# Three of sixteen pairs of k tiles in the MLP's second product done with seven block products, with the left sums on VectorE

## The chip, the cores and the metric

The kernel runs on one core of one Trainium2 chip. The metric is the device time of one execution in microseconds, as the median of several runs. A core has TensorE (matmuls; its weight loads run on a queue of their own), VectorE, ScalarE, GpSimd and SyncE, which issues most of the loads. Matmuls accumulate in PSUM, which has eight banks of 128 x 512 float32 each.

## The reference

A decoder block on 256 tokens of width 2048: a sparse attention and a Mamba-2 mixer merged by gates, an output projection, and then an MLP with 8192 hidden channels. Only the MLP's second product is done in another way here:

```python
h2 = rms_norm(x, norm2_g[l])
x = x + jnp.square(jax.nn.relu(h2 @ w_up[l])) @ w_down[l]
```

`w_up` is 2048 x 8192, `w_down` 8192 x 2048, all in float32, and the answer is wanted close to float32 accuracy.

## The kernel before

**Three matmuls for one product.** The matrices are float32; TensorE is given each operand as a high part (a copy rounded to fp32r by ScalarE, `hi`) and a low part (what is left, by VectorE, `lo`). A product of a 128 x 128 left tile by a 128 x 512 right tile is then three matmuls into the same PSUM bank: high by high, high by low, low by high. `split` (line 107) makes the two parts of a weight tile of 128 x 1024; `load` (line 115) brings the tile from HBM on SyncE's queue, into four buffers in turn; `hi` and `lo` have three buffers each.

**The MLP.** It goes in two halves of 4096 hidden channels: `up(0)`, `down(0)`, `up(1)`, `down(1)`. `up(h)` makes the hidden activations `u` (32 k tiles of 128 channels by 256 tokens) in four passes of 1024 channels. `down(h)` multiplies `u` by the matching rows of `w_down` in two passes, c2 = 0 and 1, of 1024 output columns each, over all 32 k tiles. Between a pass of `up` and the next, tasks from a queue (`u_task`) transpose the activations through an auxiliary bank; `pump` hands them out.

**The passes of `up` are mixed.** `mixed` (line 964) takes the k tiles in pairs, by the letters of `UP = "NSNSNSNN"`. With two k tiles (k), two token tiles (t) and two column halves, a pair is a 2 x 2 by 2 x 2 block product. A pair "N" takes eight products, 24 matmuls: `pieces_n` splits two weight tiles and no sums of weights are needed. A pair "S" takes seven products, 21 matmuls, by a Strassen-like scheme: `pieces_s` (line 936) needs four sums of weight blocks (`t13`, `t24`) and splits seven blocks, and the left side needs sums of the left blocks too, which `left` (line 860) makes. Seven banks q[1] to q[7] collect the products, and `combine` (line 1001) adds them up to the four output blocks at the end of the pass. In `up` the left operands (`xa`) are made once, by `norm_task`, with the left sums on GpSimd, and used by all eight passes.

**The passes of `down` are plain.** `down` (line 1079) calls `gemm_a` (line 148): for each k tile it makes the parts of `u` on the fly (`u_st`, line 1072: one ScalarE copy and one VectorE subtraction of 128 x 256, tile `uhl`), splits one weight tile and issues 4 products, 12 matmuls, into four banks. At the end of a pass one VectorE addition per bank adds the residual `xn`, into `xn` itself in `down(0)` (line 1093) and into a tile `o` in `down(1)` (line 1096), from where it goes out to HBM.

**Order.** The tile framework orders the instructions of each engine by a simulated timeline, and decides at that time which of a pool's buffers a tile gets. Seven PSUM banks are main banks, one is the auxiliary bank. Each engine then works its own list strictly in order.

Of the kernel before, what the change touches and what calls it, by code (L numbers as in the profile page):

```python
# [10 lines left out]
F32 = mybir.dt.float32  # L11
# [8 lines left out]
P = 128  # L20
# [15 lines left out]
UP = "NSNSNSNN"  # L36
NB = 32
# [9 lines left out]
def body(tc, x, x_t, vectors, taps, w_in, dt_bias, a_log, d_skip, bias_t, w_att_branch,  # L47
# [10 lines left out]
    with ctx:  # L58
# [905 lines left out]
        def mixed(kinds, w, k0, c0, operands, rate):  # L964

            q = {i: main_bank() for i in (1, 6, 7, 2, 5, 3, 4)}
            left_of = {i: sum(1 if kind == "S" else 2 * (i in LEFT_N) for kind in kinds)
# [9 lines left out]
            for j, kind in enumerate(kinds):  # L977
                hi, lo = operands(j)
                kk = k0 + 2 * j
                if kind == "S":  # L980
# [3 lines left out]
                else:  # L984
                    ws = pieces_n(w, kk, c0)
                    last = j == len(kinds) - 1
                    todo = [(i, k) for k in range(2) for i in LEFT_N]
                    if last:
                        todo.sort(key=lambda x_: list(LEFT_N).index(x_[0]))
                    for i, k in todo:  # L990
                        s_, c = LEFT_N[i]
                        s_ += 3 * k
# [8 lines left out]
        def combine(q, out_, before=None):  # L1001
# [6 lines left out]
            def with_(x_, t, c, op=OP.add):  # L1008
                if before is not None:
                    (nc.gpsimd if before[1] else v).tensor_tensor(x_, x_, before[0](t, c), op=op)  # L1010
                return x_
# [60 lines left out]
        def u_st(kk):  # L1072
            if kk == 24:
                drain()
            t = fp.tile([P, 512], F32R, name=nm("uhl"), tag="uhl", bufs=4)
            a.copy(t[:, :S], u[:, kk])
            v.tensor_tensor(t[:, S:], u[:, kk], t[:, :S].bitcast(F32), op=OP.subtract)
            return t

        def down(h):  # L1080
            for c2 in range(2):
                banks = [[main_bank(), main_bank()] for _ in range(2)]

                def d_pieces(kk):
                    hi, lo = split(load(w_down, h * MH // P + kk, 1, c2 * 1024, 1024),
                                   [P, 1, 1024])
                    return 1, hi, lo
                for t, c in gemm_a(d_pieces, MH // P, u_st, banks, 2500,
                                   tail=2 if h and c2 else 0):
                    c0 = c2 * 1024 + c * 512  # L1090
                    x_ = xn[:, t, c0:c0 + 512]
                    if h == 0:
# [56 lines left out]
```

## Time and profile before

| | |
|---|---|
| median of 3 runs | 1988.07 us (1987.48 to 1989.61) |
| the profiled execution | 1988.68 us, its span 1987.0 us |
| TensorE busy (matmul) / weight loads | 1973.6 us, 99% / 1641.5 us, 83% |
| VectorE busy | 1418.3 us, 71% |
| ScalarE busy | 1041.4 us, 52% |
| mean granted TensorE clock | 0.999 |
| up(0), down(0), up(1), down(1) begin at | 1281, 1458, 1634 and 1806 us of the span |

A busy time is the time in which an engine has an instruction under way. A matmul's shown length of some 0.39 us overlaps with the next one, so the step from one start to the next, not the length, says what a matmul costs. "Idle before, releaser" is the time an engine stood still ahead of an instruction and what it waited for.

### The profile page before, as it was taken

The numbers are of one execution on the slowest core, as the hardware profiler recorded it, in microseconds if no ns is written. First come the engines' busy times: TensorE is split into PE (matmuls) and PEld (weight loads), VectorE is DVE, ScalarE is ACT, GpSimd is POOL, SyncE is SP. The second block draws the span as 40 slices with busy tenths as digits, with TensorE's granted clock in tenths as the row PEclk, the third lists the DMA queues.
The fourth block names the chain that finished last, engine by engine and source line by source line (L and its number), as shares of the span: only waits on it lengthen the run. The fifth ranks groups of instructions, "written<-read, shape, count | busy, mean of one in ns | idle before, by whom it ended". The sixth has DMA issues, their size and how long they took to land.

```text
span 1987.0 us, 26274 instructions
## 1 busy us (share of the span) xinstructions
PE 1973.6 (99%) x9473; PEld 1641.5 (83%) x9473; DVE 1418.3 (71%) x2335; ACT 1041.4 (52%) x1566; POOL 56.8 (3%) x110
## 2 busy tenths in 40 slices
PE   8999999999999999999999999999999999999999
PEld 7878888888888888888888888778888888888887
DVE  7868656568888887888656565688855668886565
ACT  6555555444455554554554545566655445565553
POOL 2000000000000000000000000110000000000000
PEclk9999999999999999999999999999999999999999
DMA  7645555566555555565565556556656665655664
GB/s 228 209 135 183 180 168 166 161 221 191 179 182 184 187 187 185 181 187 163 179 194 188 192 190 224 179 176 205 193 189 193 194 196 190 202 190 191 192 215 145
DMA packets 132227, 372.26 MB, mean 187 GB/s; under 512 B 18288, under 2 KB 18928, under 8 KB 131840
## 3 DMA queue, kind: packets, MB, share of 16 engines
q1 hardware_dynamic: 128704, 357.87, 56.5%
q0 software_dynamic: 3248, 12.65, 2.0%
q8 instruction: 74, 1.21, 0.2%
q14 instruction: 57, 0.47, 0.1%
q10 hardware_dynamic: 144, 0.06, 0.0%
HBM read 368.37 MB, written 2.16 MB: 186 GB/s over the span
## 4 chain that ended last, share of the span: by engine, by line
PE 96%; DVE 2%; ACT 1%; DMA 1%; issue 0%; POOL 0%; SPq 0%; DVEq 0%; ACTq 0%; POOLq 0%
PE mb L152 59%; PE mb L973 15%; PE mb L126 10%; PE mb L127 5%; PE ab L747 1%; PE ab L1058 1%; PE ab L457 1%; DVE lo L111 1%; DMA raw<-in_w_in_dram 0%; PE ab L766 0%; PE ab L691 0%; PE ab L739 0%; PE ab L711 0%; PE ab L551 0%; PE ab L576 0%
## 5 line engine op out<-in xcount | busy, mean ns | idle before, releaser
L111 DVE TENSOR_TENSOR lo<-raw,hi 128x1024 fp32r<-128x1024 f32 x640 | 781.8, 1224 | 475.3 <-ACT hi L110 474.2
L110 ACT CAST hi<-raw 128x1024 fp32r<-128x1024 f32 x640 | 671.5, 1052 | 730.3 <-PE mb L152 487.4
L152 PE MATMUL mb<-hi,h_hl 128*128 128x512 f32 x1408 | 444.1, 393 | 0.0
L152 PE MATMUL mb<-hi,uhl 128*128 128x512 f32 x1024 | 315.9, 389 | 0.0
L152 PEld LDWEIGHTS mb<-hi,h_hl 128*128 128x128 f32 x1408 | 263.2, 188 | 57.1 <-issue 3.4
L152 PE MATMUL mb<-lo,h_hl 128*128 128x512 f32 x704 | 278.1, 395 | 0.3 <-DVE lo L111 0.3
L973 PE MATMUL mb<-hi,xa 128*128 128x512 f32 x832 | 263.0, 392 | 2.6 <-DVE xn L919 2.2
L126 PE MATMUL mb<-h_hl,hi 128*128 128x512 f32 x768 | 262.5, 396 | 0.0
L152 PEld LDWEIGHTS mb<-hi,uhl 128*128 128x128 f32 x1024 | 192.3, 188 | 39.8
L127 PE MATMUL mb<-h_hl,lo 128*128 128x256 f32 x768 | 204.2, 286 | 0.0
L152 PE MATMUL mb<-lo,uhl 128*128 128x512 f32 x512 | 200.0, 391 | 0.0
L973 PEld LDWEIGHTS mb<-hi,xa 128*128 128x128 f32 x832 | 156.9, 189 | 35.8 <-ACT sq L922 2.6
L126 PEld LDWEIGHTS mb<-h_hl,hi 128*128 128x128 f32 x768 | 141.9, 188 | 30.6 <-issue 1.7
L973 PE MATMUL mb<-lo,xa 128*128 128x512 f32 x416 | 164.4, 395 | 0.2
L152 PE MATMUL mb<-hi,yhl 128*128 128x512 f32 x512 | 158.0, 389 | 0.0
L152 PEld LDWEIGHTS mb<-lo,h_hl 128*128 128x128 f32 x704 | 132.3, 188 | 29.1 <-issue 1.3
L127 PEld LDWEIGHTS mb<-h_hl,lo 128*128 128x128 f32 x768 | 141.3, 189 | 5.3 <-issue 1.7
L152 PEld LDWEIGHTS mb<-hi,yhl 128*128 128x128 f32 x512 | 96.1, 188 | 20.0
L152 PEld LDWEIGHTS mb<-lo,uhl 128*128 128x128 f32 x512 | 96.1, 188 | 19.7
L152 PE MATMUL mb<-lo,yhl 128*128 128x512 f32 x256 | 99.6, 389 | 0.0
L973 PEld LDWEIGHTS mb<-lo,xa 128*128 128x128 f32 x416 | 78.4, 189 | 17.2 <-DVE lo L111 1.3
L152 PE MATMUL mb<-hi,att_hl 128*128 128x512 f32 x256 | 80.2, 392 | 0.2
(261 smaller groups left out, 2153.5 us busy)
## 6 DMA issues: line engine op xcount, KB each, us to landing
raw<-in_w_in_dram SPq DMA_DIRECT2D x286, 512.0 KB, 3.6
raw<-in_w_up_dram SPq DMA_DIRECT2D x128, 512.0 KB, 4.3
raw<-in_w_down_dram SPq DMA_DIRECT2D x128, 512.0 KB, 4.5
raw<-in_w_ssm_branch_dram SPq DMA_DIRECT2D x64, 512.0 KB, 4.4
raw<-in_w_att_branch_dram SPq DMA_DIRECT2D x32, 512.0 KB, 3.7
raw<-in_w_out_dram SPq DMA_DIRECT2D x32, 512.0 KB, 4.3
abc<-acum_d POOLq DMA_DIRECT2D x16, 512.0 KB, 5.0
bt<-in_bias_t_dram POOLq DMA_DIRECT2D x8, 256.0 KB, 2.9
```

The lines of the kernel that those rows point to most:

```text
L110: a.copy(hi, raw)
L111: v.tensor_tensor(lo, raw, hi.bitcast(F32), op=OP.subtract)
L126: pe.matmul(banks[j], hi[:, js], mv, start=kk == 0, stop=False)
L127: pe.matmul(banks[j][:, :S], lo[:, js], mv[:, :S], start=False, stop=kk == nk - 1)
L152: pe.matmul(banks[t][c], st[:, x_ + t * P:x_ + (t + 1) * P], w_[:, c * 512:(c + 1) * 512], start=kk == 0 and i == 0 and not started, stop= ...
L457: pe.matmul(bs[i][:, ds], qiT[rs_, hp, ts], kiT[rs_, ks], start=True, stop=True)
L747: pe.matmul(yd[:, i * 64:(i + 1) * 64], M[:, i], xk[c][:, i * 64:(i + 1) * 64], start=True, stop=True)
L973: pe.matmul(q[i], st, mv, start=left_of[i] == total[i] and n == 0, stop=left_of[i] == 1 and n == 2)
L1058: pe.transpose(b[:, j * S + t * P:j * S + (t + 1) * P], cs[t][c][:, f0:f0 + P], ident)
```

## The change

`down` goes through `mixed` and `combine` as `up` does. `DOWN` gives the kinds of the 16 pairs for each c2. Three pairs of each pass are "S". A new kind "P" is a plain pair whose left side needs no differences: it puts the two diagonal terms into bank 2 and a new bank 8. "N" needs one difference of left blocks. Bank 8 is the auxiliary bank, taken at the first "P" pair of a pass. The left operands of `down` are made anew for every pair of each pass (`u_operands`, tiles `ah` and `al`, two buffers each). `left` makes its sums on VectorE in place of GpSimd, for `up` too; the sums for "S" are three instructions in place of four. `combine` has the residual to add in, and where bank 8 is in use, one more block (`w4`).

```diff
+DOWN = ('NNSNNPPSPPPPSPPP', 'PPSPPPPSPPPPSPPP')
...
+        LEFT_P = {2: (0, 0), 8: (1, 1), 3: (0, 1), 4: (1, 0)}
+        SLOTS = {"S": 7, "N": 6, "P": 4}
...
             if kind == "S":
-                a11, a12, a21, a22 = src[:, 0, 0], src[:, 1, 0], src[:, 0, 1], src[:, 1, 1]
-                g.tensor_tensor(d[:, 1], a21, a22, op=OP.subtract)
-                g.tensor_tensor(d[:, 2], d[:, 1], a11, op=OP.subtract)
-                g.tensor_tensor(d[:, 0], d[:, 2], a12, op=OP.add)
-                g.tensor_tensor(d[:, 3], a11, a21, op=OP.subtract)
-                parts = ((slice(0, 2), src[:, :, 0]), (2, a22), (slice(3, 7), d))
-            else:
-                g.tensor_tensor(d[:, :2], src[:, :, 0], src[:, :, 1], op=OP.subtract)
+
+                d = pool.tile([P, 4, P], F32, name=nm("d"), tag="d", bufs=2)
+                v.tensor_tensor(d[:, :2], src[:, 0], src[:, :, 1], op=OP.subtract)
+                v.tensor_tensor(d[:, 2], d[:, 1], src[:, 0, 0], op=OP.subtract)
+                v.tensor_tensor(d[:, 3], d[:, 2], src[:, 1, 0], op=OP.add)
+                parts = ((slice(0, 2), src[:, :, 0]), (2, src[:, 1, 1]), (slice(3, 7), d))
+            elif kind == "N":
+                d = pool.tile([P, 4, P], F32, name=nm("d"), tag="d", bufs=2)
+                v.tensor_tensor(d[:, :2], src[:, :, 0], src[:, :, 1], op=OP.subtract)
                 hi, lo = (z.rearrange("p (k n) t -> p k n t", n=3) for z in (hi, lo))
                 parts = (((slice(None), slice(0, 2)), src), ((slice(None), 2), d[:, :2]))
+            else:
+                parts = ((slice(0, 4), src.rearrange("p k h t -> p (k h) t")),)
...
+                if kind == "P" and q[8] is None:
+                    q[8] = aux_bank()
...
-                (nc.gpsimd if before[1] else v).tensor_tensor(w3, u3, before[0](1, 1),
-                                                              op=OP.subtract)
-                v.tensor_tensor(out_[1][1], q[5], w3, op=OP.subtract)
+                v.tensor_tensor(w3, u3, before(1, 1), op=OP.subtract)
+                if 8 in q:
+                    w4 = block()
+                    v.tensor_tensor(w4, q[8], w3, op=OP.subtract)
+                    v.tensor_tensor(out_[1][1], q[5], w4, op=OP.add)
+                else:
+                    v.tensor_tensor(out_[1][1], q[5], w3, op=OP.subtract)
...
-        def u_st(kk):
-            if kk == 24:
-                drain()
-            t = fp.tile([P, 512], F32R, name=nm("uhl"), tag="uhl", bufs=4)
-            a.copy(t[:, :S], u[:, kk])
-            v.tensor_tensor(t[:, S:], u[:, kk], t[:, :S].bitcast(F32), op=OP.subtract)
-            return t
+        u4 = u.rearrange("p k (t n) -> p k t n", t=2)
 
         def down(h):
+            def u_operands(j):
+                if kinds[j] == "P" or 2 * j == 24:
+                    drain()
+                n = SLOTS[kinds[j]]
+                hi = fp.tile([P, n, P], F32R, name=nm("ah"), tag="ah", bufs=2)
+                lo = fp.tile([P, n, P], F32R, name=nm("al"), tag="al", bufs=2)
+                left(kinds[j], fp, u4[:, 2 * j:2 * j + 2], hi, lo)
+                return hi, lo
+
             for c2 in range(2):
-                banks = [[main_bank(), main_bank()] for _ in range(2)]
...
-                for t, c in gemm_a(d_pieces, MH // P, u_st, banks, 2500,
-                                   tail=2 if h and c2 else 0):
...
+                kinds = DOWN[c2]
+                q = mixed(kinds, w_down, h * MH // P, c2 * 1024, u_operands, 5000)
...
+                combine(q, new, old)
+                if h:
+                    for t, c in ((0, 0), (1, 1), (0, 1), (1, 0)):
+                        o0 = c2 * 1024 + c * 512
+                        nc.sync.dma_start(out2[t * P:(t + 1) * P, o0:o0 + 512], new[t][c])
```

Over the whole program TensorE's list goes from 8992 to 8956 rows, VectorE's from 2047 to 2177, GpSimd's loses its 17 left sums, and SyncE's keeps 709. Three places in the lists follow.

VectorE, the last "S" pair of the last pass, where the list before has four plain k tiles. Before (`uhl` is the low part of one k tile of `u`, `lo` that of a weight tile):

```order
L1077 TENSOR_TENSOR uhl_17239<-u,uhl_17239 128x256
L111 TENSOR_TENSOR lo_17236<-raw_17233,hi_17235 128x1024
L1077 TENSOR_TENSOR uhl_17260<-u,uhl_17260 128x256
L111 TENSOR_TENSOR lo_17257<-raw_17254,hi_17256 128x1024
L1077 TENSOR_TENSOR uhl_17281<-u,uhl_17281 128x256
```

Now (`al` is the low part of the left blocks, `d` a left sum, `t` a sum of weight blocks, `l` and `lo` low parts of weights):

```order
L955 TENSOR_TENSOR t_3550_17436<-raw_17424 128x512
L883 TENSOR_TENSOR al_17373<-u,ah_17372 128x512
L112 TENSOR_TENSOR lo_17379<-raw_17376,hi_17378 128x1024
L952 TENSOR_TENSOR l_3547_17429<-raw_17424,h_3546_17428 128x512
L956 TENSOR_TENSOR t_3550_17436<-raw_17424,raw_17426 128x512
L959 TENSOR_TENSOR t_3553_17443<-t_3550_17436,raw_17426 128x512
L112 TENSOR_TENSOR lo_17385<-raw_17382,hi_17384 128x1024
L960 TENSOR_TENSOR t_3553_17443<-t_3553_17443,raw_17426 128x512
L883 TENSOR_TENSOR al_17413<-u,ah_17412 128x256
L883 TENSOR_TENSOR al_17413<-u,ah_17412 128x128
L883 TENSOR_TENSOR al_17413<-d_17414,ah_17412 128x512
L112 TENSOR_TENSOR lo_17433<-raw_17426,hi_17432 128x1024
```

The sums of weights of the "S" pair stand among the splits of the "P" pair ahead of it (`lo_17379`, `lo_17385`), so VectorE begins on an "S" pair one pair early.

TensorE, the change from c2 = 0 to c2 = 1 of `down(0)`. Before (`mb` is a main bank):

```order
L152 MATMUL mb_13164<-lo_13847,uhl_13850 128x512
L152 MATMUL mb_13164<-hi_13846,uhl_13850 128x512
L152 MATMUL mb_13869<-hi_13875,uhl_13879 128x512
L152 MATMUL mb_13870<-hi_13875,uhl_13879 128x512
L152 MATMUL mb_13871<-hi_13875,uhl_13879 128x512
```

Now (`ab_13937` is bank 8 of the new pass, which is the auxiliary bank; the first row here is the sixteenth of the new pass):

```order
L981 MATMUL mb_13931<-hi_13946,al_13934 128x512
L981 MATMUL mb_13932<-lo_13947,ah_13933 128x512
L981 MATMUL mb_13932<-hi_13946,al_13934 128x512
L981 MATMUL ab_13937<-hi_13940,ah_13933 128x512
L981 MATMUL ab_13937<-lo_13941,ah_13933 128x512
```

The new pass opens with 18 matmuls into three main banks (`mb_13929`, `mb_13931`, `mb_13932`); its products for bank 8 come behind them.

VectorE, the end of the program. Before:

```order
L111 TENSOR_TENSOR lo_17371<-raw_17368,hi_17370 128x1024
L1096 TENSOR_TENSOR o_17383<-mb_16725,xn 128x512
L1096 TENSOR_TENSOR o_17392<-mb_16726,xn 128x512
L1096 TENSOR_TENSOR o_17401<-mb_16727,xn 128x512
L1096 TENSOR_TENSOR o_17410<-mb_16728,xn 128x512
```

Now (`ev` is a block of `combine`):

```order
L112 TENSOR_TENSOR lo_17564<-raw_17561,hi_17563 128x1024
L1028 TENSOR_TENSOR o_17591<-mb_16889,ev_17595 128x512
L1037 TENSOR_TENSOR ev_17607<-ab_16897,ev_17605 128x512
L1038 TENSOR_TENSOR o_17594<-mb_16890,ev_17607 128x512
L1041 TENSOR_TENSOR o_17592<-mb_16891,ev_17603 128x512
L1042 TENSOR_TENSOR o_17593<-mb_16892,ev_17599 128x512
```

Five instructions stand behind the last split in place of four; the other seven of `combine` have moved ahead of it.

## Rows read from the trace of the kernel before

**Rows 1.** The page: busy time of the engines, and the chain that ended last by engine.

```profile
PE 1973.6 (99%) x9473; PEld 1641.5 (83%) x9473; DVE 1418.3 (71%) x2335; ACT 1041.4 (52%) x1566; POOL 56.8 (3%) x110
...
PE 96%; DVE 2%; ACT 1%; DMA 1%; issue 0%; POOL 0%; SPq 0%; DVEq 0%; ACTq 0%; POOLq 0%
```

**Rows 2.** Who waited for whom in down(0), 1458 to 1634 us: engine, line and tile that waited, what it waited for, us in total, times, longest us.

```profile
ACT hi L110 <- PE mb L152: 80.3, 59, 3.4
DVE lo L111 <- ACT hi L110: 69.8, 59, 2.2
```

**Rows 3.** The same view of up(1), 1634 to 1806 us.

```profile
ACT hi L110 <- PE mb L973: 33.9, 27, 2.2
DVE lo L111 <- ACT hi L110: 18.1, 20, 1.9
...
PEld mb L973 <- DVE lo L111: 0.4, 1, 0.4
```

**Rows 4.** The chain that ended last, in order of time, from up(0)'s end on: start us, us, what, how many. L152 is a matmul of `down`, L973 one of `up`, L1058 a transpose of `u_task`.

```profile
1458.02 6.12 PE mb L152 x27
...
1470.28 0.44 PE ab L1058 x4
...
1482.13 151.90 PE mb L152 x670
1634.03 47.38 PE mb L973 x209
...
1806.15 6.12 PE mb L152 x27
...
1830.26 150.56 PE mb L152 x664
```

**Rows 5.** Busy time of the engines by stretch (start:end us, length, then busy us and instructions of each engine, granted TensorE clock, DMA share, GB/s): a pass of up(0), down(0), up(1), down(1).

```profile
1380.90:1424.30 43.40, 43.40 (x201) 35.85 (x200) 36.19 (x42) 26.54 (x32) 0.00 (x0) 1.00 0.61 194
...
1458.00:1634.00 176.00, 176.00 (x786) 145.73 (x785) 105.17 (x137) 90.50 (x133) 0.00 (x0) 1.00 0.60 190
1634.00:1806.10 172.10, 172.08 (x782) 141.87 (x781) 142.44 (x165) 100.99 (x119) 0.00 (x0) 1.00 0.59 197
1806.10:1987.00 180.90, 176.06 (x785) 145.43 (x783) 103.23 (x135) 87.89 (x130) 0.00 (x0) 0.99 0.58 184
```

**Rows 6.** VectorE's instructions from 1230 us on, by line and shape: out and in shapes, count, busy us, mean ns of one, idle before.

```profile
L111 DVE TENSOR_TENSOR lo<-raw,hi 128x1024 fp32r<-128x1024 f32 x248 | 303.7, 1227 | 188.3 <-ACT hi L110 187.9
L1077 DVE TENSOR_TENSOR uhl<-u,uhl 128x256 fp32r<-128x256 f32 x128 | 53.2, 417 | 0.0
L959 DVE TENSOR_TENSOR l<-t,h 128x1024 fp32r<-128x1024 f32 x24 | 29.2, 1218 | 0.0
...
L947 DVE TENSOR_TENSOR l<-raw,h 128x512 fp32r<-128x512 f32 x24 | 16.5, 688 | 8.0 <-ACT h L946 8.0
...
L955 DVE TENSOR_TENSOR t<-t,raw 128x512 f32<-128x512 f32 x24 | 16.4, 682 | 0.0
...
L1096 DVE TENSOR_TENSOR o<-mb,xn 128x512 f32<-128x512 f32 x8 | 5.0, 681 | 4.5 <-PE mb L152 4.5
...
L878 DVE TENSOR_TENSOR xa<-xf,xa 128x128 fp32r<-128x128 f32 x3 | 1.4, 456 | 0.0
...
L1031 DVE TENSOR_REDUCE rstd<-ssq 128x1 f32<-128x4 f32 x2 | 0.3, 148 | 0.0
```

**Rows 7.** The instructions in order of time at the change from the second to the third pass of up(0): start us, us, engine, line, what, how many in a run. L1017, L1020, L1026 and L1027 are the four closing additions of `combine`.

```profile
1370.76 1.07 PE L973 MATMUL mb<-hi,xa 128*128 128x512 f32 x4
...
1372.30 0.69 DVE L1017 TENSOR_TENSOR c<-mb,ev 128x512 f32<-128x512 f32 x1
...
1372.80 1.07 PE L973 MATMUL mb<-hi,xa 128*128 128x512 f32 x4
...
1373.71 0.39 PE L973 MATMUL mb<-lo,xa 128*128 128x512 f32 x1
...
1375.83 0.68 DVE L1026 TENSOR_TENSOR c<-mb,ev 128x512 f32<-128x512 f32 x1
...
1376.43 0.68 DVE L1027 TENSOR_TENSOR c<-mb,ev 128x512 f32<-128x512 f32 x1
```

**Rows 8.** The end of the program in order of time, the same columns; SPq is SyncE's DMA issue.

```profile
1980.84 2.48 DVE L1096 TENSOR_TENSOR o<-mb,xn 128x512 f32<-128x512 f32 x4 [4.49 <-PE mb L152]
...
1981.56 2.12 SPq L1097 DMA_DIRECT2D out_dram<-o  x4
1981.77 0.39 PE L152 MATMUL mb<-hi,uhl 128*128 128x512 f32 x1
```

**Rows 9.** TensorE's instructions in order of time at the start of up(0), columns as in group 7.

```profile
1278.40 0.39 PE L152 MATMUL mb<-hi,mhl 128*128 128x512 f32 x1
1280.96 0.47 PE L973 MATMUL mb<-hi,xa 128*128 128x512 f32 x1 [2.17 <-DVE xn L919]
```

**Rows 10.** Busy time by stretch there, columns as in group 5.

```profile
1281.00:1286.00 5.00, 5.00 (x15) 3.98 (x16) 4.58 (x12) 2.39 (x8) 0.00 (x0) 0.66 0.23 54
1286.00:1291.00 5.00, 5.00 (x25) 4.12 (x25) 4.51 (x10) 4.28 (x8) 0.85 (x1) 1.00 0.53 188
```

**Rows 11.** GpSimd's left sums, all in 1241 to 1310 us: line, count, duration in ns min/median/max, first and last start.

```profile
L872 POOL TENSOR_TENSOR d<-xf x5: 740/1167/1272, 1241.3 to 1308.4; 128x256 f32<-128x256 f32 x5
...
L867 POOL TENSOR_TENSOR d<-d,xf x3: 461/521/3064, 1246.1 to 1298.3; 128x128 f32<-128x128 f32 x3
```

**Rows 12.** VectorE in order of time in up(0)'s first pass, columns as in group 7: where it waited for such a sum's ScalarE copy.

```profile
1302.57 0.69 DVE L878 TENSOR_TENSOR xa<-d,xa 128x512 fp32r<-128x512 f32 x1 [1.55 <-ACT xa L877]
```

More of the change, by code (lines that the diff above doesn't have):

```diff
@@ L966, in mixed @@
             q = {i: main_bank() for i in (1, 6, 7, 2, 5, 3, 4)}
-            left_of = {i: sum(1 if kind == "S" else 2 * (i in LEFT_N) for kind in kinds)
+            if "P" in kinds:
+                q[8] = None
+            lefts = {"S": LEFT_S, "N": LEFT_N, "P": LEFT_P}
+            left_of = {i: sum((1 if kind == "S" else 2) * (i in lefts[kind]) for kind in kinds)
                        for i in q}
@@ L986, in mixed @@
                     last = j == len(kinds) - 1
-                    todo = [(i, k) for k in range(2) for i in LEFT_N]
+                    at = lefts[kind]
+                    todo = [(i, k) for k in range(2) for i in at]
                     if last:
-                        todo.sort(key=lambda x_: list(LEFT_N).index(x_[0]))
+                        todo.sort(key=lambda x_: list(at).index(x_[0]))
                     for i, k in todo:
-                        s_, c = LEFT_N[i]
-                        s_ += 3 * k
+                        s_, c = at[i]
+                        s_ += SLOTS[kind] // 2 * k
                         cs = slice(c * 512, c * 512 + 512)
@@ L1009, in with_ @@
                 if before is not None:
-                    (nc.gpsimd if before[1] else v).tensor_tensor(x_, x_, before[0](t, c), op=op)
+                    v.tensor_tensor(x_, x_, before(t, c), op=op)
                 return x_
@@ L1070, in up @@
                 queue.append(u_task(g, cs))
-        def u_st(kk):
-            if kk == 24:
-                drain()
-            t = fp.tile([P, 512], F32R, name=nm("uhl"), tag="uhl", bufs=4)
-            a.copy(t[:, :S], u[:, kk])
-            v.tensor_tensor(t[:, S:], u[:, kk], t[:, :S].bitcast(F32), op=OP.subtract)
-            return t
-        def down(h):
-            for c2 in range(2):
-                banks = [[main_bank(), main_bank()] for _ in range(2)]
[L1084 to L1087, printed above, removed]
-                for t, c in gemm_a(d_pieces, MH // P, u_st, banks, 2500,
-                                   tail=2 if h and c2 else 0):
-                    c0 = c2 * 1024 + c * 512
-                    x_ = xn[:, t, c0:c0 + 512]
-                    if h == 0:
-                        v.tensor_tensor(x_, banks[t][c], x_, op=OP.add)
-                        continue
-                    o = fp.tile([P, 512], F32, name=nm("o"), tag="c", bufs=4)
-                    v.tensor_tensor(o, banks[t][c], x_, op=OP.add)
-                    nc.sync.dma_start(out2[t * P:(t + 1) * P, c0:c0 + 512], o)
@@ new lines, in body, with old @@
+        u4 = u.rearrange("p k (t n) -> p k t n", t=2)
+        def down(h):
+            def u_operands(j):
[6 more added lines that the diff above has]
+                return hi, lo
+            for c2 in range(2):
+                kinds = DOWN[c2]
+                q = mixed(kinds, w_down, h * MH // P, c2 * 1024, u_operands, 5000)
+                def old(t, c):
+                    return xn[:, t, c2 * 1024 + c * 512:c2 * 1024 + c * 512 + 512]
+                if h == 0:
+                    new = [[old(t, c) for c in range(2)] for t in range(2)]
+                else:
+                    new = [[fp.tile([P, 512], F32, name=nm("o"), tag="c", bufs=4)
+                            for _ in range(2)] for _ in range(2)]
+                combine(q, new, old)
[3 more added lines that the diff above has]
+                        nc.sync.dma_start(out2[t * P:(t + 1) * P, o0:o0 + 512], new[t][c])
```

4 lines of the change are left out of this document (1 added, 3 removed).

## The prediction

> **What bounds the kernel now.** I read the page first. TensorE is busy for 1973.6 of 1987.0 us, and 96% of the chain that ended last is its own [rows 1]. A matmul's shown length overlaps with the next one, so a busy share alone could hide room; the views of waits and of the chain decide. In down(0) the only long waits are ScalarE's for a bank of weight parts that TensorE has still to finish with (80.3 us) and VectorE's for ScalarE (69.8 us) [rows 2]: both are early, and TensorE never waits. In up(1), where "S" pairs already stand, TensorE's one wait is 0.4 us [rows 3]. The chain gives the price of a matmul: 151.90 us for 670 and 150.56 us for 664, both 0.2267 us each; four transposes take 0.44 us [rows 4]. So each matmul less is worth 0.2267 us, as long as VectorE keeps ahead. It is busy for 105.17 of 176.0 us in down(0) and for 142.44 of 172.1 us in up(1) [rows 5].
>
> **The change part by part.**
>
> *Matmuls.* An "S" pair has 21 matmuls, the plain pair 24, and "N" and "P" keep 24. With 3 "S" in each of four passes that is 12 x 3 = 36 less, as the lists of the two programs show (8992 rows to 8956). 36 x 0.2267 = 8.2 us, all on the path.
> The Trainium skill (TensorE: Matmul & The Clock Gate, Back-to-back issue gap) gives some 131 ns for a 512-column matmul in a stream with its weight load. By that figure the saving would be an estimated 36 x 0.131 = 4.7 us and the end 3.5 us later than I forecast; the step of 0.2267 us in the chain does not bear it out.
>
> *VectorE in `down`.* Durations from the trace: 1.22 us for 128x1024, 0.69 for 128x512, 0.42 for 128x256 [rows 6]. No row here shows 128x128 undisturbed: it lies between 0.148 (one column) and 0.456 us (a row beside GpSimd's work); a line through the 256 and 512 rows gives 0.28, which I take.
> "S" pair, left: one sum of 256 and two of 128, low parts of 256, 128 and 512: 0.42 + 0.56 + 0.42 + 0.28 + 0.69 = 2.4 us. Weights: five of 512 and three of 1024, 3.45 + 3.66 = 7.1 us. Together 9.5 us, against 21 x 0.2267 = 4.8 us of TensorE. "P": 0.69 + 2 x 1.22 = 3.1 us against 5.4. "N" adds a sum and a part of 256 each: 4.0 us. The closing additions are twelve of 0.68 where there were four, 8.2 us. A pass with c2 = 0 has 3 S, 4 N and 9 P: 28.5 + 16.0 + 27.9 + 8.2 = 80.6 us; c2 = 1 has 3 S and 13 P: 77.0 us. TensorE takes 375 x 0.2267 = 85.0 us for either. So VectorE goes from 60% to at most 93%; since back-to-back instructions start some 8% sooner than their lengths say (1375.83 and 1376.43 for two of 0.68) [rows 7], 85% is nearer. Still under TensorE, and up(1) ran at 83% with 0.4 us of waits.
>
> *Around one "S".* The 4.7 us by which it exceeds TensorE must be done ahead. Each "P" leaves 2.3 us. The list puts the weight sums of an "S" among the splits of the "P" before it, its buffers `h1`, `h4` and `t13` are its own, and its last parts are wanted only after 3 to 6 of its 7 products, 2 to 4 us into it. With one "P" ahead and those 2 to 4 us inside it comes out about even, and two or more "P" or "N" pairs follow each time, where VectorE recovers. In up(1) "S" and "N" alternate, and the same sums go: 172.1 us for 732 matmuls (165.9 us) and 12 groups of transposes (5.3 us) leave 0.9 us, some 0.08 us for each of 12 "S" pairs; down(0) leaves 176.0 - 768 x 0.2267 - 4 x 0.44 = 0.1 us [rows 4, 5]. Bounds for the four new passes: nothing, and 4 us (0.33 for each "S"). I take 1.2 us, up(1)'s excess and a little for the fuller VectorE.
>
> *Change of pass.* `combine` holds seven banks. At such a change in up(0) TensorE ran on at its step while the additions read the old banks from 1372.30 to 1377.1, for the first products of the new pass go to three banks already free [rows 7]. In the new list a `down` pass opens with 18 matmuls (4.1 us) into three main banks too, and bank 8, of which there is one, comes behind. Its reader `w4` is the second closing instruction: finished some 1.3 us after the pass ends, 2.8 us early. I cost the change of pass at nothing; if VectorE were 3 us late there, TensorE would stand.
>
> *ScalarE* copies what VectorE subtracts and makes none of the sums: 5.7 us for an "S" at VectorE's durations, 3.1 us for a "P". It waited 80.3 us for buffers in down(0) [rows 2], which covers it. The loads are the same 128 tiles in the same order; 190 GB/s in `down` rises by 2% [rows 5].
>
> *The end.* In the profiled run the closing additions start 0.93 us before the last matmul and run back to back for 2.48 us, and the last store follows [rows 8]. Now five stand there: one more at a step of 0.60 us, so +0.6 us. The other seven are ahead of the last splits.
>
> *Left sums of `up` on VectorE.* GpSimd's sums took 0.46 to 3.06 us each [rows 11], and one chain of them cost VectorE a wait of 1.55 us [rows 12]; VectorE gets some 5 us more to do, half of it in the first pass, where it is nearly full. TensorE hardly waits there. Between -1 and +1 us; I take nothing.
>
> *Sum.* -8.2 + 1.2 + 0.6 = -6.4 us. From the profiled execution's 1988.68 us that is 1982.3; the median before lies 0.6 us under that execution, so 1981.7 us.
>
> **The rivals.**
> A. *VectorE becomes the bound at the "S" pairs* (the other side). If only one "P" pair's slack of 2.3 us counts, an "S" stalls TensorE for 2.4 us: 12 x 2.4 = 29 us, 1988.1 - 7.6 + 29 = 2010 us. It takes 7.6 / 12 = 0.63 us a pair to give back all, 1.0 us to be slower by over 0.2%. For it: 9.5 us against 4.8, and two pairs only of buffered weights. Against: up(1)'s 0.08 us.
> B. *A gap at the change of pass, and the clock.* Ahead of up(0) TensorE stood from 1278.4 to 1280.96 [rows 9], and in the 5 us after it the granted clock averaged 0.66, thus in part at 1.2 GHz, with 15 matmuls where 22 fit (5 / 0.2267) [rows 10]: 2.6 + 1.6 = 4.2 us. If `w4` or a late split makes such a gap where c2 changes, once in each half, the time is 1981.7 + 8.4 = 1990.1 us, with one 1985.9. For it: one auxiliary bank, VectorE full. Against: the 2.8 us in hand.
> The Trainium skill (TensorE: Matmul & The Clock Gate, What's actually happening) says of the clock that "the default state is throttled, and activity releases the throttle". [...]
> C. *A matmul less is worth less than its step*, because the stream is paced by something else than the matmuls: at half the step, 1985.8 us. Against it: the 21- and 24-matmul pairs of up(1) together have the step of the plain ones in `down`, within the 0.9 us above.
> D. *The first pass of up(0) gains* from sums without GpSimd: up to 2.4 us, 1979.3 us. VectorE's wait of 1.55 us speaks for it, TensorE's small waits against.
>
> That the change does not do what it says is excluded by the count of rows.
>
> **How the numbers follow.** Forecast 70%, with its own range 1979.8 to 1984.0 (stalls of 0 to 3.5 us). B 14%, A 8%, C 4%, D 4%. The range that holds 8 in 10 takes in D's end and one gap of B: 1979.5 to 1986.5. A measurement here can tell 0.2%, 4 us: faster means under 1984.1. Faster: forecast, D and a part of B, 0.76; same: most of B, C and a part of A, 0.16; slower 0.08.
>
> **What would show it.** Matmuls of `down` at a step of 0.2267 us, and down(0) at about 172.5 us in place of 176.0 (18 matmuls less, 0.6 us of stalls); VectorE at 85 to 93% there; no TensorE wait on `l` or `lo` over 0.3 us; granted clock 1.00; five closing instructions at the end. Wrong: TensorE waits on VectorE in an "S" pair of over 0.6 us each, a gap of over 2 us at a change of c2 with a lower clock behind it, or a span in up(0) that moves by more than 1 us.

## The result, and the profile after

| | before | after |
|---|---|---|
| median, same chip | 1988.61 us (1987.48 to 1990.11, 5 runs) | 1978.54 us (1978.02 to 1980.81, 5 runs) |
| profiled execution / its span | 1988.68 / 1987.0 us | 1978.39 / 1976.3 us |

The ratio is 0.995, with an interval of 0.9936 to 0.9965. The kernel is 10.1 us faster. Forecast were 6.4 us, and 1978.54 us lies under the lower end of the range, 1979.5 us. The five runs of the kernel before are the three of the table ahead of the prediction and two more.

Where the 10.7 us between the two spans went, by the first matmul of each stage and the last matmul of the program:

| stage | before | after | difference |
|---|---|---|---|
| up to the first matmul of up(0) | 1280.96 | 1280.30 | -0.66 |
| up(0) | 176.89 | 174.45 | -2.44 |
| down(0) | 176.02 | 171.93 | -4.09 |
| up(1) | 172.12 | 171.77 | -0.35 |
| down(1), to the start of its last matmul | 175.78 | 172.02 | -3.76 |
| from there to the end of the span | 5.23 | 5.83 | +0.60 |

The page after, which answers to [rows 1]:

```profile
PE 1963.7 (99%) x9437; PEld 1633.8 (83%) x9437; DVE 1500.6 (76%) x2465; ACT 1063.6 (54%) x1562; POOL 38.2 (2%) x93
...
PE 98%; DVE 1%; ACT 1%; DMA 0%; issue 0%; SPq 0%; DVEq 0%; ACTq 0%
```

The trace has 36 matmuls less (9473 to 9437, the very 12 x 3), and VectorE 82 us more. TensorE's share of the chain rose from 96 to 98%: there is less waiting in the chain, though VectorE is fuller.

Busy time by stretch after, columns as in [rows 5]: a pass of up(0), down(0), up(1), and from down(1) to the end; then the two stretches of [rows 10].

```profile
1374.40:1417.70 43.30, 43.30 (x199) 35.30 (x198) 35.92 (x42) 25.94 (x32) 0.00 (x0) 1.00 0.60 194
1454.80:1626.70 171.90, 171.90 (x768) 142.34 (x767) 143.32 (x188) 101.52 (x131) 0.00 (x0) 1.00 0.62 195
1626.70:1798.40 171.70, 171.70 (x781) 141.97 (x780) 144.88 (x172) 101.30 (x119) 0.00 (x0) 1.00 0.61 197
1798.40:1976.30 177.90, 172.46 (x767) 142.09 (x766) 142.36 (x187) 98.66 (x128) 0.00 (x0) 1.00 0.58 187
...
1281.00:1286.00 5.00, 5.00 (x24) 4.05 (x24) 4.50 (x15) 3.32 (x6) 0.00 (x0) 1.00 0.28 67
1286.00:1291.00 5.00, 5.00 (x26) 4.17 (x25) 4.11 (x7) 4.42 (x8) 0.00 (x0) 1.00 0.44 147
```

In down(0) TensorE is busy in 171.90 of 171.90 us: it doesn't stand once, with VectorE at 143.32 us, 83%, where it had 60%. In down(1) it waits once for a low part, which costs 0.3 us:

```profile
1891.88 0.19 PEld L981 LDWEIGHTS mb<-lo,ah 128*128 128x128 f32 x1 [0.42 <-DVE lo L112]
```

And in 1281 to 1286 us the granted clock is 1.00 and 24 matmuls fit, where before it was 0.66 with 15.

The longest waits of down(0), 1454.75 to 1626.7 us, columns as in [rows 2]:

```profile
ACT ah L882 <- PE mb L981: 32.9, 27, 1.8
ACT hi L111 <- PE mb L981: 25.7, 24, 1.7
DVE lo L112 <- ACT hi L111: 14.1, 23, 1.7
ACT h L951 <- DMA raw<-in_w_down_dram: 7.2, 5, 3.4
DVE t L955 <- DMA raw<-in_w_down_dram: 7.0, 6, 2.4
```

The 80.3 us that ScalarE waited for TensorE have shrunk to 58.6 us in two lines, and VectorE's 69.8 us for ScalarE to 14.1 us in one. No row of this stage has TensorE in front. New are waits for a weight tile at the first instructions of an "S" pair (L951 and L955 are in `pieces_s`).

### The profile page after: what moved, and what is told of

Read it like the earlier page. It is cut to its first block, busy times and chain, and to the rows that moved or that the text cites. A ratio compares the mean times of both kernels' runs of the same rounds, so it can differ in the third digit from the quotient of the medians.

```text
span 1976.3 us, 26219 instructions
## 1 busy us (share of the span) xinstructions
PE 1963.7 (99%) x9437; PEld 1633.8 (83%) x9437; DVE 1500.6 (76%) x2465; ACT 1063.6 (54%) x1562; POOL 38.2 (2%) x93
## 4 chain that ended last, share of the span: by engine, by line
PE 98%; DVE 1%; ACT 1%; DMA 0%; issue 0%; SPq 0%; DVEq 0%; ACTq 0%
PE mb L153 42%; PE mb L981 31%; PE mb L127 10%; PE mb L128 5%; PE ab L981 3%; PE ab L748 1%; PE ab L1073 1%; PE ab L458 1%; PE ab L692 0%; PE ab L767 0%; PE ab L740 0%; PE ab L712 0%; DMA raw<-in_w_in_dram 0%; PE ab L552 0%; PE ab L577 0%; PE ab L573 0%
## 5 line engine op out<-in xcount | busy, mean ns | idle before, releaser
L112 DVE TENSOR_TENSOR lo<-raw,hi 128x1024 fp32r<-128x1024 f32 x628 | 765.5, 1222 | 361.1 <-ACT hi L111 359.3
L111 ACT CAST hi<-raw 128x1024 fp32r<-128x1024 f32 x628 | 658.1, 1052 | 619.5 <-PE mb L153 329.1
L981 PE MATMUL mb<-lo,ah 128*128 128x512 f32 x376 | 146.7, 391 | 0.0
L981 PE MATMUL mb<-hi,al 128*128 128x512 f32 x376 | 146.1, 389 | 0.0
L981 PE MATMUL mb<-hi,ah 128*128 128x512 f32 x376 | 122.1, 390 | 0.0
L981 PEld LDWEIGHTS mb<-lo,ah 128*128 128x128 f32 x376 | 70.6, 188 | 15.0 <-DVE lo L112 0.4
L981 PEld LDWEIGHTS mb<-hi,al 128*128 128x128 f32 x376 | 70.6, 188 | 14.4
```

The costliest lines, as they stand in the source:

```text
L111: a.copy(hi, raw)
L112: v.tensor_tensor(lo, raw, hi.bitcast(F32), op=OP.subtract)
L981: pe.matmul(q[i], st, mv, start=left_of[i] == total[i] and n == 0, stop=left_of[i] == 1 and n == 2)
```

## The experiments

Each ran on one chip beside the kernel before. Ratios are to that.

### One and five S pairs in each pass of `down`

```diff
-DOWN = ('NNSNNPPSPPPPSPPP', 'PPSPPPPSPPPPSPPP')
+DOWN = ('NNSNNPPPPPPPPPPP', 'PPPPPPSPPPPPPPPP')    # s1
+DOWN = ('NNSNPSPPSPPSPPSP', 'PSPPSPPSPPSPPSPP')    # s5
```

> One S pair a pass in place of three, everything else as in the changed kernel: 8 S pairs and 24 matmuls are given back. If TensorE's step alone sets the price of an S pair (0.68 us each, no stalls): 8 x 0.68 = 5.4 us slower than the changed kernel, 1984.0 us, with down(0) at 174.6 us. If an S pair's heavier VectorE list costs something (the prediction's 0.1 us a pair, or more): the loss is smaller, 4.6 us or less, 1983 us.

> Five S pairs a pass in place of three. If TensorE stays the bound: 8 S pairs and 24 matmuls more saved, 5.4 us faster than the changed kernel, 1973.1 us. If VectorE becomes the bound: its busy time in a pass of down was 71 us with three S pairs and each S adds about 5.7, so 82 us against TensorE's 83.6; then TensorE waits on low parts, down(0) stays at 172 us or gets longer, and the time is 1978 us or more.

Measured: one a pass 1985.47 us, 0.9984 (0.9975 to 0.9992); five 1991.04 us, 1.0011 (1.0002 to 1.002). With 0.2267 us for each matmul less than the 176.02 us of before, down(0) would take 174.66, 171.94 and 169.22 us with one, three and five "S" pairs a pass. It took 174.65, 171.93 and 176.78 us, of which the last holds three matmuls of up(1) that ran ahead, 0.68 us. So up to three each pair is worth its three matmuls to 0.01 us in down(0), and at five 6.9 us of stalls eat more than the 6.8 us that were saved there. (The 10.7 us that the expectation for four pairs below speaks of add the waits of weight loads and of matmuls at the same places.) With one pair a pass the program lost 6.9 us to the changed kernel, not the 5.4 of the step alone; the two down stages lost 5.1 us by their profiles, and the rest lies in up(0) (175.45 us, behind a clock of 0.70) and up(1) (172.57 us).

Busy time in down(0) with five, columns as above, and who waited there:

```profile
1455.60:1632.40 176.80, 172.95 (x758) 139.64 (x757) 160.55 (x228) 108.31 (x146) 0.00 (x0) 1.00 0.60 189
```

```profile
ACT h L951 <- DMA raw<-in_w_down_dram: 25.4, 10, 3.8
...
DVE t L955 <- DMA raw<-in_w_down_dram: 12.2, 8, 2.6
...
PEld mb L981 <- DVE lo L112: 7.2, 10, 2.2
PE mb L981 <- DVE lo L112: 3.5, 5, 1.8
```

VectorE is at 91%, not 100%, in the stage in which TensorE waits for it: it stood for tiles itself (12.2 us). A mean share does not tell the limit.

### Three S pairs in a row

```diff
+DOWN = ('NNNNNPPSSSPPPPPP', 'PPPPPPPSSSPPPPPP')    # clump
```

> Three S pairs a pass as in the changed kernel, but next to each other (places 7 to 9). Matmuls and VectorE's total are the same. If only the total counts: 1978.5 us. If an S pair must be prepared ahead (the prediction's working around one S: 9.5 us by durations, about 8.5 by starts, against 4.8): the first S is covered by the lead, the second and third wait some 3 us each, 4 to 7 us a pass, 16 to 28 us in all: 1994 to 2006 us, with waits of TensorE on low parts in this one place of each pass.

Measured: 1999.74 us, 1.0051 (1.0039 to 1.0064), within the 1994 to 2006 us that preparing an "S" ahead gave. The stages `down` took 182.24 and 181.74 us, 10.3 and 9.7 us more than in the changed kernel, with the same matmuls. The stretch around the three in the first pass, TensorE's waits:

```profile
1505.98 0.73 PE L981 MATMUL mb<-h,ah 128*128 128x512 f32 x2 [0.25 <-ACT h L963]
1507.38 0.50 PE L981 MATMUL mb<-lo,ah 128*128 128x512 f32 x1 [0.67 <-DVE lo L112]
1509.18 0.50 PE L981 MATMUL mb<-l,ah 128*128 128x512 f32 x1 [0.62 <-DVE l L952]
1511.99 0.49 PE L981 MATMUL mb<-lo,ah 128*128 128x512 f32 x1 [0.47 <-DVE lo L112]
1515.67 0.50 PE L981 MATMUL mb<-hi,al 128*128 128x512 f32 x1 [0.88 <-DVE al L883]
```

All lie within 10 us. TensorE's time over its step of 0.2267 us is 5.0 us from 1502 to 1516 us, around the three "S" pairs of the first pass, and 5.0 us from 1593 to 1606 us, around those of the second: nearly all that the stage lost. VectorE's whole work in down(0) was 144.49 us there, about what the changed kernel has. So the spacing is what makes the change free: the excess of an "S" on VectorE is real, and the plain pairs ahead and behind hide it.

### Four S pairs, in three placements

```diff
+DOWN = ('NNSNNPSPPSPPSPPP', 'PSPPPSPPPSPPPSPP')    # s4
+DOWN = ('NNSNNPSPPSPPSPPP', 'PPPSPPSPPSPPSPPP')    # s4_late
+DOWN = ('NNSNNPSPPSPPSPPP', 'PPSPPPPSPPPPSPPP')    # s4_s3: 4 and 3
```

> Four S pairs a pass. The runs with one and three S pairs gave down(0) exactly the step times the matmuls left (174.65 and 171.93 us); with five, TensorE waited 10.7 us on VectorE's low parts and down(0) came out at 176.8. If the limit is VectorE's total (151 us of work in 170 us by the slope of these runs, under 100%): no waits, 2.7 us faster than the changed kernel, 1975.8 us, down(0) 169.9 us. If the limit is the work between two S pairs (P pairs give back 2.4 us each of the 3.6 to 4.7 that an S pair needs, so two P pairs per S are too few as in the run with five): where only two P pairs stand between, waits come up; down(0) 170 to 173 us, and the time 1976 to 1980 us.

> Four S pairs a pass as in the run before with four, but in the passes of the second half (c2 = 1) at places 3, 6, 9 and 12, so that none stands directly behind the closing work of the pass before. Theory 1 (the stalls came from an S queued behind that closing work): no stall in either pass, the down stages are 176.02 - 24 x 0.2267 = 170.6 us each, and the program is 2 x 1.36 = 2.7 us faster than the changed kernel, about 1975.8 us. Theory 2 (four S pairs in 85 us are too many for VectorE wherever they stand): the down stages stay at about 175.4 us as in the run with four, and the program at about 1985.5 us.

> Four S pairs in the passes of the first half (places 2, 7, 10, 13, unchanged from the run with four, which had no stall there) and three, as in the changed kernel, in the passes of the second half (places 2, 7, 12). Theory 1 (the number in a pass isn't the limit, the closing work ahead of an S is): the down stages are 176.02 - 21 x 0.2267 = 171.3 us and the program 1.3 us faster than the changed kernel, about 1977.2 us. Theory 2 (a pass with four leaves VectorE late for the next pass): stalls at the start of the second half, down stages at 173 us or more, program at 1981 us or more.

| | median us | ratio (interval) | down(0) | down(1) | down(0) without stalls |
|---|---|---|---|---|---|
| s4 | 1985.54 | 0.9982 (0.9973 to 0.9991) | 175.41 | 175.42 | 170.58 |
| s4_late | 1979.4 | 0.9954 (0.9942 to 0.9967) | 170.92 | 173.35 | 170.58 |
| s4_s3 | 1978.86 | 0.9951 (0.9939 to 0.9964) | 171.91 | 171.47 | 171.26 |

In s4 down(0) holds 0.68 us of matmuls of up(1), as with five pairs, and down(1), which is counted to the start of its last matmul, would take 0.24 us less than down(0) without stalls. In down(0) of s4 the first pass had 0.2 us of stalls; the second had the rest, from its first "S" on, at place 1:

```profile
1543.30 0.69 DVE L955 TENSOR_TENSOR t<-raw 128x512 f32<-128x512 f32 x1 [3.78 <-DMA raw<-in_w_down_dram]
...
1547.98 0.68 DVE L1028 TENSOR_TENSOR xn<-mb,ev 128x512 f32<-128x512 f32 x1
...
1553.25 0.68 DVE L1038 TENSOR_TENSOR xn<-mb,ev 128x512 f32<-128x512 f32 x1
```

VectorE stood 3.78 us for the tile and then had the "S" sums and the closing additions of the pass (L1028 to L1042) to do together, until 1553.9 us; in the changed kernel these are done by 1545.9. In s4_late the first "S" of the pass stands two places later (and two of the others one place off), and 3.8 us of the 4.1 us of stalls in down(0) were gone. This bears out that an "S" close behind a change of pass stalls. But in down(1) of the same kernel 3.0 us stayed, spread over 1897 to 1947 us, 13 us and more behind the change of pass at 1884 us. VectorE's longest wait there:

```profile
1943.33 0.69 DVE L955 TENSOR_TENSOR t<-raw 128x512 f32<-128x512 f32 x1 [3.10 <-DMA raw<-in_w_down_dram]
```

So the theory that only the place counts fell in part. VectorE was busy for 151.5 us in down(0) of this kernel, with 0.3 us of stalls, and for 149.9 us in down(1), with 3.0: the total does not tell them apart. None of the three is shown to beat the changed kernel: the intervals of the two that come near overlap with its own, and s4 is slower.

### A fifth buffer for weight tiles

```diff
-RAW = 4
+RAW = 5
...
-                d = pool.tile([P, 4, P], F32, name=nm("d"), tag="d", bufs=2)
+                d = pool.tile([P, 4, P], F32, name=nm("d"), tag="d", bufs=2 if pool is mp else 1)
```

> The lists of the last run with four S pairs in every pass, with five buffers for arriving weight tiles in place of four (all through the program), and one buffer in place of two for the left sums d of the MLP, which makes the room. Theory 1 (an S pair finds VectorE idle because its weight tile has not arrived, 11.9 us of such waits in down(1) of that run, since SyncE may not start a load before VectorE is done with one of four tiles; VectorE's total is not the limit): the waits for DMA shrink by half or more, the stalls of 2.8 us in down(1) go, both down stages come to 170.6 us, and the program, the stages before the MLP unchanged, to about 1976 us. Theory 2 (VectorE's own instructions around an S pair set the time, and it waits for a tile only because nothing else is ready): the down stages stay at 171 and 173 us and the program within 1 us of 1979.4 us. The stages before the MLP also get the fifth buffer; what the first matmul of up(0) shows later or earlier than 1280.8 us is theirs and belongs to neither theory.

Measured: 1991.52 us, 1.0013 (1.0004 to 1.0022), 12 us slower than with four buffers. The waits that should have halved did not, in down(1), 1806.5 to 1983.7 us:

```profile
ACT h L951 <- DMA raw<-in_w_down_dram: 21.5, 7, 5.2
...
DVE t L955 <- DMA raw<-in_w_down_dram: 9.4, 6, 2.4
```

Without the edit these two were 25.2 and 11.9 us. Neither theory had foreseen the loss, which lies in the `down` stages (178.7 and 177.2 us) for the most part. The longest single stall, 2.5 us at 1495.8 us, follows on a wait of ScalarE of 5.6 us for a weight tile of an "S" pair: the tile came late with five buffers too. The edit also moved the order of the whole program, and left `d` one buffer, so what made it slower is not told apart; and why a tile comes late to an "S" where a pass has four of them stays open.

### The left sums alone, both ways

```diff
-            g = nc.gpsimd
+            g = v                  # before_dve: the kernel before, sums on VectorE
...
-                left(UP[j], scratch[0], x_, z[:, :, :P], z[:, :, P:])
+                left(UP[j], scratch[0], x_, z[:, :, :P], z[:, :, P:], nc.gpsimd)   # pool_sums: after, sums of up on GpSimd
```

> The kernel before with nothing changed but the engine of the left sums of up: VectorE in place of GpSimd. Theory 1 (the sums): 2 to 2.5 us faster than before, 1986.2 us. Theory 2 (the clock behind the gap): 1988 us, as before within 0.7 us, with the same split by the mean granted clock.

> The changed kernel with the left sums of up back on GpSimd (the sums of down stay on VectorE). Theory 1, that up(0) got 2.4 us shorter because GpSimd's slow sums left its first pass: the time goes up by 2 to 2.5 us to 1980.5 to 1981 us, at a granted clock of 1.000 too. Theory 2, that the 2.4 us are the granted clock, which fell behind the gap at the start of up(0) in the profiled run of before and did not in that of the changed kernel: no change of the median beyond 0.7 us, and runs with a mean clock of 0.998 to 0.999 are some 2 us slower than runs with 1.000 of the same kernel.

Measured: 1987.0 us for the kernel before with sums on VectorE, 0.9992 (0.9983 to 1.0001), and 1980.51 us for the changed kernel with them on GpSimd, 0.9959 (0.9947 to 0.9972). The second is what theory 1 gave, the first lies between the two theories. Medians: 1.4 us gained, and 2.0 us lost, by the same step in the two directions. Neither is certain by the intervals alone: the first interval includes a ratio of 1, the second overlaps with the changed kernel's. The profiles show the stage more sharply:

| | sums of `up` on | clock in 1281 to 1286 us | up(0) |
|---|---|---|---|
| before | GpSimd | 0.66 | 176.89 |
| pool_sums | GpSimd | 1.00 | 176.97 |
| s1, s5, s4, s4_s3, s4_raw5, clump, last_n | VectorE | 0.66 to 0.75 | 175.45 to 176.13 |
| after, before_dve, s4_late | VectorE | 1.00 | 174.45, 174.16, 173.86 |

With GpSimd's sums up(0) takes 176.9 us whether the clock falls at its start or not. In pool_sums it didn't fall, and TensorE waited later on:

```profile
1302.16 0.50 PE L981 MATMUL mb<-h,xa 128*128 128x512 f32 x1 [0.20 <-ACT h L951]
1305.85 0.50 PE L981 MATMUL mb<-lo,xa 128*128 128x512 f32 x1 [0.47 <-DVE lo L112]
1334.28 0.74 PE L981 MATMUL mb<-hi,xa 128*128 128x512 f32 x2 [0.40 <-ACT hi L111]
```

GpSimd's sums there, by line and shape (count, busy us, mean ns of one):

```profile
L871 POOL TENSOR_TENSOR d<-d,xf 128x128 f32<-128x128 f32 x3 | 5.1, 1706 | 0.2
...
L869 POOL TENSOR_TENSOR d<-xf 128x256 f32<-128x256 f32 x3 | 3.8, 1252 | 8.9 <-ACT xf L907 8.9
L870 POOL TENSOR_TENSOR d<-d,xf 128x128 f32<-128x128 f32 x3 | 2.8, 932 | 0.2
```

The 128 x 128 operations of L870 and L871, which took 0.28 and 0.29 us on VectorE in the changed kernel, took 0.93 and 1.71 us on GpSimd. One late sum holds up what stands behind it in ScalarE's list: ScalarE waits for the sum, and its next copy is the high part of a weight (`h`) that TensorE waits for in the first row above.

```profile
1297.86 3.07 POOL L871 TENSOR_TENSOR d<-d,xf 128x128 f32<-128x128 f32 x1
...
1300.96 0.62 ACT L882 CAST xa<-d 128x512 fp32r<-128x512 f32 x1 [3.08 <-POOL d L871]
1301.49 0.61 ACT L951 CAST h<-raw 128x512 fp32r<-128x512 f32 x1
```

Both kernels have the same 732 products in up(0). Set product against product, TensorE in pool_sums is even with the changed kernel up to the 80th, 1.0 us behind it at the 100th, 2.1 us at the 250th (1342 us), and 2.5 us at the last. TensorE of the kernel before is 1.6 us behind already at the 15th, under the fallen clock, 1.8 us at the 100th, 2.9 us at the 250th and 2.45 us at the last. So in these two profiles the two costs cover each other in part: a TensorE that is late by the lower clock meets fewer of the waits that GpSimd's sums bring, and each shows its full price only when the other is gone.

The medians by the mean granted clock of a run say nearly the same, on one chip: the kernel before took 1988.1 us at 1.0 (10 runs) and 1988.9 us at 0.999 (16 runs), before_dve 1985.9 us (3 runs) and 1987.5 us (8 runs). At either clock the move is worth 1.4 us or more, which the clock can't explain; and a lower mean clock costs 1.6 us with the sums on VectorE against 0.8 us before. In pool_sums it costs nothing that five runs show.

### The gap ahead of up(0)

The main pool is closed there and opened anew with seven banks, and TensorE waits for its last readers (`xn`) [rows 9]. After, in the same place:

```profile
1277.74 0.39 PE L153 MATMUL mb<-hi,mhl 128*128 128x512 f32 x1
1280.30 0.47 PE L981 MATMUL mb<-hi,xa 128*128 128x512 f32 x1 [2.17 <-DVE xn L924]
```

Two kernels leave the pool as it was, so that only six main banks and two auxiliary ones are there; one takes bank 4 of each pass from the auxiliary ones, the other bank 1:

```diff
-        psum_stack.close()
-        psum[:] = [enter(tc.tile_pool(name="psum2", bufs=1, space=PSUM)), 7]
...
-            q = {i: main_bank() for i in (1, 6, 7, 2, 5, 3, 4)}
+            q = {i: main_bank() for i in (1, 6, 7, 2, 5, 3)}      # one_pool
+            q[4] = aux_bank()
...
+            q = {i: main_bank() for i in (6, 7, 2, 5, 3, 4)}      # one_pool_q1: q[1] = aux_bank() at the first S
```

> The changed kernel without the change of PSUM pool ahead of up(0): the first pool of six main and two auxiliary banks stays, and bank 4 of a mixed pass comes from the auxiliary ones. This takes away TensorE's gap of 2.3 us there. If the gap is the new pool's wait for the last readers of the old one: 2.3 us less in every run, and 1.5 us more in those runs in which the clock fell behind the gap; granted clock 1.000 in all runs; 1976 us. If the tighter auxiliary banks cost as much at the changes of pass, the time stays at 1978.5 us or rises.

> The changed kernel without its change of the PSUM pool: seven banks in the main pool all through, and in down the eighth bank, which the 7-product pairs alone need (the sum of block product 1), comes from the auxiliary pool at the first such pair, instead of bank 4 from the start. Theory 1 (the run with bank 4 from the auxiliary pool gave its gain at the start of up(0) back, because its plain pairs in down waited for that pool): the gap at the start stays gone (start at about 1278.0 us), down stages at 171.9 us as in the changed kernel, program at 1977.5 us or less. Theory 2 (what the gap costs is given back inside up(0) whatever the pools are, by waits for GpSimd and ScalarE): up(0) again about 175.6 us and the program within 0.5 us of the changed kernel's 1978.5 us.

The second expectation speaks of seven main banks; in the kernel as it ran there are six and two auxiliary ones, and bank 1, which only the 7-product pairs need, comes from the latter in `up` as well.

Measured: 1978.81 us, 0.9948 (0.9935 to 0.996), and 1979.64 us, 0.9953 (0.9939 to 0.9966): the changed kernel's own time, within what can be told, and not the 1976 to 1977.5 us that a gap simply taken away would give. The gap is gone in both, but up(0) took 175.58 and 178.16 us in place of 174.45, and in the first the `down` stages took 172.42 and 172.97 us in place of 171.93 and 172.02, which gives the 2.3 us back. The profiled run of the second is the slowest of its five (1981.21 us; the lowest is 1978.07). In it TensorE ran into ScalarE's copies instead, in 1295 to 1310 us (who waited for whom, us in total, times, longest):

```profile
PE mb L980 <- ACT h L961: 1.7, 1, 1.7
PE ab L980 <- ACT h L949: 0.3, 1, 0.3
```

and the granted clock fell there (busy time by stretch, columns as in [rows 5]):

```profile
1296.00:1300.00 4.00, 4.00 (x20) 3.29 (x19) 4.00 (x8) 3.23 (x5) 0.00 (x0) 1.00 0.47 131
1300.00:1304.00 4.00, 1.98 (x7) 1.05 (x6) 4.00 (x7) 2.82 (x4) 0.00 (x0) 0.92 0.44 127
1304.00:1308.00 4.00, 4.00 (x13) 3.16 (x12) 4.00 (x7) 1.35 (x2) 0.00 (x0) 0.65 0.77 217
```

VectorE is busy throughout these 12 us. A TensorE that does not stand for 2.3 us ahead of the stage comes nearer to what the other engines prepare, and in this run it waited there.

### The end

```diff
+DOWN = ('NNSNNPPSPPPPSPPP', 'PPSPPPPSPPPPSPPN')    # last_n
```

> The changed kernel with the last pair of c2 = 1 plain of kind N in place of P, so that bank 8 is finished a pair earlier and w4 can be made before the end. If the end is set by the closing instructions: four in place of five stand behind the last matmuls, and the stretch from the last matmul's start to the end of the span goes from 5.83 back to 5.2 us; the time falls by 0.6 us at most, 1978.0 us. If it is set by the stores, no change.

Measured: 1983.19 us, 0.997 (0.9959 to 0.9981), slower than the changed kernel in all six runs (1982.51 us and more against 1980.81 and less). I had expected fewer closing additions behind the last matmul; there were nine. An "N" as last pair leaves bank 5 open to the end, and `ev` and its successors hang on it. From the last matmul's start to the end of the span it took 8.15 us in place of 5.83, about 4 x 0.6 = 2.4 us for four more. That is a little under half of the 5.1 us between the two profiled spans. The kind of the last pair holds for down(0) too: there as well nine closing additions stand behind the last matmul, until 1640 us, and TensorE waits at the start of up(1), which took 173.09 us in place of 171.77. The other 1.4 us are in up(0) (175.81 us), behind a clock of 0.66.

## Why the prediction was wrong in its size

The mechanism came as forecast, and two terms of the sum were mis-sized, so that it fell 3.7 us short (3.2 us by the predicted time itself, since the median of the kernel before rose by 0.5 us with the two further runs). By the profiled spans it fell 4.3 us short: 2.44 in up(0), 0.85 in the two `down` stages, 0.66 ahead of up(0) and 0.35 in up(1). Step by step:

*Matmuls*, -8.2 us. Right: 36 less, 0.2267 us each, to 0.01 us in down(0). The 131 ns that I quoted from the Trainium skill (TensorE: Matmul & The Clock Gate, Back-to-back issue gap) would have made this saving an estimated 4.7 us; s1 and the changed kernel show the whole step of 0.2267 us for each, so the figure does not hold for this stream. Rival C falls with it.

*Stalls at the "S" pairs*, "I take 1.2 us, up(1)'s excess and a little for the fuller VectorE": this term failed. It measured 0.3 us: nothing in down(0), 171.93 us where 171.94 are the matmuls and transposes, and the one wait of down(1). I had read the 0.9 us of up(1) as stalls of its "S" pairs. Only 0.30 us of it was a stall, the one wait for a low part of [rows 3], at 1742 us; the rest is time between matmuls and transposes that my figures for the two leave out. In the changed kernel that wait is gone, and up(1), with the same pairs, takes 0.35 us less. The ledger for VectorE, 157.6 us for the two passes by lengths, measured 143.3: 83%, nearer to my 85 than to the 93. (The two rows that I took 8% from, 0.60 us apart for a length of 0.68, give 12%.)

*Left sums of `up` on VectorE*, "Between -1 and +1 us; I take nothing": this failed too, and it is the larger part. The step is worth 1.4 to 2.0 us by the medians of the two kernels that make it alone, and 2.5 us in up(0) where the clock did not fall, outside my bounds. I had the evidence in front of me, the 3.06 us for a GpSimd sum and VectorE's wait of 1.55 us [rows 11, 12], and set it aside because TensorE's own waits in the stage looked small. They were, behind the start of the stage: one wait of a matmul of 0.40 us, at 1335.26 us, is named in the trace of before. But the 2.44 us between the two profiles are not the sums alone. 1.6 us were lost in the first 15 products, in 1281 to 1285.4 us, at steps of up to 0.43 us under the fallen clock, which no row of waits shows, and 1.1 us at 1329 and 1335 us, where pool_sums loses the same; 0.4 us came back later in the stage. That the clock fell in the profiled run of before was luck, which no term of the sum held; pool_sums shows that with the sums on GpSimd the stage takes as long without the fall. My own sign of an error, a span in up(0) that moves by more than 1 us, came true with 2.44. Rival D named this mechanism, with up to 2.4 us and 1979.3 us, and got 4%. It came together with the forecast, not in place of it; taking the two for alternatives kept the sum of both out of my range: with 0.3 us of stalls and 2.0 us for the sums it is 1981.7 - 0.9 - 2.0 = 1978.8 us.

*The end*, +0.6 us. Right: 5.23 to 5.83 us, five closing additions 0.6 to 0.7 us apart.

```profile
1969.53 0.69 DVE L1028 TENSOR_TENSOR o<-mb,ev 128x512 f32<-128x512 f32 x1 [4.49 <-PE mb L981]
...
1970.14 0.68 DVE L1037 TENSOR_TENSOR ev<-ab,ev 128x512 f32<-128x512 f32 x1
...
1970.25 2.85 SPq L1114 DMA_DIRECT2D out_dram<-o  x4
...
1970.86 0.69 DVE L1038 TENSOR_TENSOR o<-mb,ev 128x512 f32<-128x512 f32 x1
1971.47 0.68 DVE L1041 TENSOR_TENSOR o<-mb,ev 128x512 f32<-128x512 f32 x1
1972.06 0.68 DVE L1042 TENSOR_TENSOR o<-mb,ev 128x512 f32<-128x512 f32 x1
```

*Change of pass*, nothing. Right. Closing additions and TensorE between the passes of down(0):

```profile
1541.99 0.68 DVE L1037 TENSOR_TENSOR ev<-ab,ev 128x512 f32<-128x512 f32 x1
...
1545.23 0.68 DVE L1038 TENSOR_TENSOR xn<-mb,ev 128x512 f32<-128x512 f32 x1
```

```profile
1541.68 0.84 PE L981 MATMUL mb<-hi,ah 128*128 128x512 f32 x3
...
1545.76 0.39 PE L981 MATMUL ab<-hi,ah 128*128 128x512 f32 x1
1545.99 0.39 PE L981 MATMUL ab<-lo,ah 128*128 128x512 f32 x1
```

L1037 reads bank 8 (`ab`) until 1542.7 us, and the first matmul that needs it comes 4.1 us after the pass began, 3.1 us later: the 2.8 us in hand were real.

*Rival A* did not come about at three, and its mechanism is real: with the same count in a row or with five a pass TensorE waits for VectorE's low parts, and the kernel is slower than before. The point that I gave, 0.63 us a pair, was the right kind of bound: at five the 6.9 us in down(0) are 0.69 us for each of ten, just over the 0.68 us that a pair saves. *Rival B* fell: no gap at a change of c2, and a clock of 1.00.

The 0.66 us by which up(0) starts earlier have no cause that a run here shows; starts lay between 1280.0 and 1281.5 us in the kernels that reopen the pool. My own range of the forecast, 1979.8 to 1984.0 us, doesn't follow from its terms either: with no stalls at all the sum gives 1980.5 us.

## What to carry to other kernels

Where the busiest engine is bound by its own instruction step, price a removed instruction at that step, as long as the helper engine's excess is spaced so that its neighbours can absorb it. In this kernel the spacing, not the mean busy share, decided when it stopped being free (143 us of VectorE's work in a stage of 172 us cost nothing spaced, 144 us with three "S" pairs in a row cost 10 us). A side effect of a change (here the move of some sums to another engine) is to be summed with the main term, not listed as a rival to it. What a stage loses is best measured against count x step, or product against product of two kernels: a lowered clock has no row of waits.

## What the runs showed of the hardware

The gap of 2.33 us ahead of up(0) is in all kernels that reopen the pool, but the granted clock behind it differed: 0.66 in 1281 to 1286 us before and in s4, s4_s3, s4_raw5 and last_n, 0.70 in s1 and s5, 0.75 in clump, 1.00 in after, pool_sums, before_dve and s4_late. Where it fell, six or seven matmuls behind the gap came 0.427 us apart in place of 0.2267. The changed kernel's own five runs have a mean clock of 1.0 or 0.998, with 1978.0 to 1978.5 us in the three of the first kind and 1978.9 and 1980.8 in the others. With the sums on VectorE a fall cost up(0) about 1 to 2 us (175.45 to 176.13 against 173.86 to 174.45), and with GpSimd's sums nothing that the two profiles show (176.89 and 176.97). What decides whether it falls, the runs don't show.
